# Linear recurrence layer: casts of x and of weights moved from ScalarE to VectorE, and gate weights loaded a step earlier

## The chip, the cores and the metric

One core of one Trainium2 chip runs the whole program. The metric is device microseconds (us) of one execution, as the median of several runs. Five queues work side by side: PE (TensorE, matmuls; PEld its weight loads), DVE (VectorE), ACT (ScalarE), POOL (GpSimd) and SP (SyncE, which here only issues DMAs). Each takes its instructions in a fixed order and stands at the first one that has to wait.

## What is computed

The reference runs four layers over 256 context tokens and 512 latent tokens of width 1024: rwkv7, rglru (a gated linear recurrence), natten, rwkv7. Only the second, rglru, is changed. Cut to its core:

```python
z = h @ w_in                          # 1024 -> 2 * 1408
xr, g = z[..., :1408], z[..., 1408:]
x = depthwise_conv_centred(xr, conv_w, conv_b)     # 4 taps over time
for d in range(2):                    # forward, backward
    r = sigmoid(block_diag(x, gate_w[d, 0]) + gate_b[d, 0])   # 16 blocks of 88
    i = sigmoid(block_diag(x, gate_w[d, 1]) + gate_b[d, 1])
    log_a = -8 * r * softplus(-lam[d])
    a, b = exp(log_a), sqrt(-expm1(2 * log_a)) * (i * x)
    h_d = linear_scan(a, b)           # context first, then latents
y = ((h_0 + h_1) * silu(g)) @ w_out   # 1408 -> 1024
```

## The kernel before

Every large fp32 matmul is made of three. A matrix is split into a high part (a cast to fp32r) and a low part (the source less the high part, cast again), and the sum of high*high, low*high and high*low is taken. So each operand costs a cast (hi) and a subtraction (lo). The helper `split` (L224) does this for activations and gate weights, `load_w` (L208) for projection weights. Before, the cast of both stands on ACT (`nc.scalar.copy`, L227 and L218) and the subtraction on DVE (L230, L221).

The layer has 1408 channels in 11 blocks of 128, all 768 tokens in the free dimension. Names of tiles as the profile shows them: `wr` a raw weight, `wh`, `wl` its parts; `xf` a projection's result, `xc` the convolved x, `xh` its two parts; `ha` the two parts of a halo (rows of the two neighbour blocks that an 88-wide gate block reaches into); `gr` a raw gate weight, `gh`, `glo` its parts; `sg`, `aa` the gates and the recurrence; `gt` the silu gate; `pa`, `pb` PSUM banks (four of each kind).

Two streams of work are written one into the other by `merge` (L130, called at L1536): `projs`, the 22 projection tiles in the order of `LRO` (x0 x1 x2 g0 x3 g1 x4 g2 ... x10 g8 g9 g10), eight k-steps of six matmuls each (L1402), and `units`, six units of two blocks (the last of one). A unit first makes its gates, four steps (block, gate) with two directions each (L1486, then a sigmoid on ACT that empties the banks, L1492), and then its tail: tanh, exp and square root on ACT (L1497, L1502, L1505), then on DVE the products and scans (L1509 to L1516), one addition on POOL (L1518), a product (L1519) and the store of z.

The order on ACT is the order as written (`manual_schedule` of ACT, L1533). The other queues are put in order by a list scheduler, by readiness in its own time model and else as written. `ahead` at the third k-step of a tile (L1398) loads and splits the weight of the next tile. `xtile` (L1405) copies its result out of PSUM on ACT, convolves on DVE (L1416, L1418) and splits x; at every even block it also fetches the halo of the block before by two DMAs and splits it.

`gw_in(i)` (L1456) loads and splits the gate weight of step i; it is called for step i+1 in the middle of step i, between the two directions, two or three DMAs of 128 KB each. Raw gate tiles and raw projection weights share one ring of three buffers (tag `wr`); `gh`, `glo`, `wh` and `wl` have two each. `self.hi_dve = (0, 1)` (L156) and the counter `self.alt` decide in `load_w` where a weight's cast goes: with (0, 1) always to ACT.

After the last unit the output projection (`out_proj`, L373) loads z and its own weights; its first matmul is at L244.

Of the kernel before, what the change touches and what calls it, by code (L numbers as in the profile page):

```python
# [10 lines left out]
F32 = mybir.dt.float32  # L11
# [5 lines left out]
P = 128  # L17
# [107 lines left out]
def run_all(gen):  # L125
    for _ in gen:
        pass
# [22 lines left out]
class Build:  # L150
# [1197 lines left out]
    def rglru(self, li, pv, md, xs, acc, xsp, last):  # L1348

        tc, nc, a = self.tc, self.nc, self.a  # L1350
        NT = 11
        toks = [(0, TC), (TC, TL)]
        HSEG = ((2, TC), (260, TL))
# [32 lines left out]
        self.pq = tc.alloc_tile_pool(name=f"lps{li}", bufs=4, space=bass.MemoryType.PSUM)  # L1386
        order = [(c[0], int(c[1:])) for c in LRO.split()]
        self.plan([(a[f"l{li}_win"][m + NT * (c == "g")], 1024) for c, m in order])
        self.ahead(2)
# [3 lines left out]
        def dense(m):  # L1393
            wh, wl = self.need()
            outs = [self.psa(), self.psa()]
            for kt in range(KT):
                if kt == 2:
                    self.ahead()  # L1398
                ws = slice(kt * 128, kt * 128 + 128)
                for p_i, (wt, xt) in enumerate(((wh, h[kt][0]), (wl, h[kt][0]), (wh, h[kt][1]))):  # L1400
                    for pt, (s0, n) in zip(outs, SEGS):
                        nc.tensor.matmul(pt[:, :n], wt[:, ws], xt[:, s0:s0 + n], start=(kt == 0 and p_i == 0), stop=(kt == KT - 1 and p_i == 2))  # L1402
                yield outs

        def xtile(m):  # L1405

            for outs in dense(m):
                yield 1.0
            xp = self.g("xf")
            for z in (0, 258, 772):  # L1410
                nc.gpsimd.memset(xp[:, z:z + 2], 0.0)
            for pt, o0, n in ((outs[0], 2, TC), (outs[1], 260, TL)):
                nc.scalar.copy(xp[:, o0:o0 + n], pt[:, :n])
            x = xc[m] = self.g("xc")
            cw = lambda j: pv[:, self.LRU_CW + j * NT + m:self.LRU_CW + j * NT + m + 1]
            nc.vector.tensor_scalar(x[:, 2:772], xp[:, 0:770], cw(0), pv[:, self.LRU_CB + m:self.LRU_CB + m + 1], op0=ALU.mult, op1=ALU.add)  # L1416
            for j in range(1, 4):
                nc.vector.scalar_tensor_tensor(out=x[:, 2:772], in0=xp[:, j:j + 770], scalar=cw(j), in1=x[:, 2:772], op0=ALU.mult, op1=ALU.add)  # L1418
            hi, lo = X[m] = self.g("xh", F32R), self.g("xh", F32R)
            self.split(x[:, 2:772], hi[:, 2:772], lo[:, 2:772])  # L1420
            if m and m % 2 == 0:

                r1, r2 = halo(m - 1)
                n, xf = r1 + r2, self.g("xf")
                nc.sync.dma_start(xf[0:r1, 2:772], xc[m - 2][P - r1:P, 2:772])
                nc.sync.dma_start(xf[r1:n, 2:772], x[0:r2, 2:772])
                hi, lo = X["n", m - 1] = self.g("ha", F32R), self.g("ha", F32R)
                self.split(xf[:n, 2:772], hi[:n, 2:772], lo[:n, 2:772])

        first = [xtile(0), xtile(1)]  # L1430

# [10 lines left out]
        def gtile(m):  # L1442

            for outs in dense(NT + m):
                yield 1.0
# [5 lines left out]
        base = [0]  # L1451
        for m in range(NT):
            base.append(base[-1] + len(gate_src(m)))
        GW = {}

        def gw_in(i):  # L1456

            if i < 2 * NT:
                m, gi = divmod(i, 2)
                n = (base[m + 1] - base[m]) * 256  # L1460
                gr = self.wp.tile([P, 768], F32, tag="wr", name=self.nm("gr"), bufs=self.wb[0])
                gh = self.gp.tile([P, 768], F32R, tag="gh", name=self.nm("gh"), bufs=2)
                gl = self.gp.tile([P, 768], F32R, tag="gl", name=self.nm("glo"), bufs=2)
                for s_ in range(base[m + 1] - base[m]):
                    nc.sync.dma_start(gr[:, s_ * 256:s_ * 256 + 256], a[f"l{li}_gw"][base[m] + s_, gi])
                self.split(gr[:, :n], gh[:, :n], gl[:, :n])
                GW[i] = gh, gl

        def unit(ms):

            self.mark(f"unit{ms[0]}")
            keys = [(m, d) for m in ms for d in range(2)]
            R, I, A = {}, {}, {}
            for m in ms:
                srcs = gate_src(m)
                for gi, dstt in ((0, R), (1, I)):
                    if 2 * m + gi == 0:
                        gw_in(0)
                    gh, gl = GW.pop(2 * m + gi)
                    for d in range(2):  # L1480
                        outs = [self.psb(), self.psb()]
                        for si, (key, k) in enumerate(srcs):
                            ws = slice(si * 256 + d * 128, si * 256 + d * 128 + 128)
                            for p_i, (wt, xt) in enumerate(((gh, X[key][0]), (gl, X[key][0]), (gh, X[key][1]))):
                                for pt, (s0, n) in zip(outs, HSEG):
                                    nc.tensor.matmul(pt[:, :n], wt[:k, ws], xt[:k, s0:s0 + n], start=(si == 0 and p_i == 0), stop=(si == len(srcs) - 1 and p_i == 2))  # L1486
                        if d == 0:
                            gw_in(2 * m + gi + 1)
                        o = dstt[m, d] = self.g("sg")
                        cb = self.LRU_GB + (d * 2 + gi) * NT + m  # L1490
                        for pt, (s0, n) in zip(outs, toks):
                            nc.scalar.activation(o[:, s0:s0 + n], pt[:, :n], AF.Sigmoid, bias=pv[:, cb:cb + 1])  # L1492
                        yield float(len(srcs))

            for m, d in keys:
                A[m, d] = self.g("aa")
                nc.scalar.activation(A[m, d][:, :T], R[m, d][:, :T], AF.Tanh, scale=spl[:, d * NT + m:d * NT + m + 1])  # L1497
                for (s0, n), (x0, _) in zip(toks, HSEG):
                    (nc.gpsimd if d else nc.vector).tensor_tensor(out=I[m, d][:, s0:s0 + n], in0=I[m, d][:, s0:s0 + n], in1=xc[m][:, x0:x0 + n], op=ALU.mult)
                yield 0.3  # L1500
            for m, d in keys:
                nc.scalar.activation(R[m, d][:, :T], R[m, d][:, :T], AF.Exp, scale=spn[:, d * NT + m:d * NT + m + 1])  # L1502
                yield 0.3
            for m, d in keys:
                nc.scalar.activation(A[m, d][:, :T], A[m, d][:, :T], AF.Sqrt)  # L1505
            yield 1.0
            for m, d in keys:
                aa, bb, hs = R[m, d], A[m, d], I[m, d]
                nc.vector.scalar_tensor_tensor(out=bb[:, :T], in0=aa[:, :T], scalar=1.0, in1=bb[:, :T], op0=ALU.add, op1=ALU.mult)  # L1509
                nc.vector.tensor_tensor(out=bb[:, :T], in0=bb[:, :T], in1=hs[:, :T], op=ALU.mult)  # L1510
                if d == 0:
                    nc.vector.tensor_tensor_scan(out=hs[:, :T], data0=aa[:, :T], data1=bb[:, :T], initial=0.0, op0=ALU.mult, op1=ALU.add)
                else:
                    rv = lambda ap, s0, n: ap[:, s0:s0 + n][:, ::-1]
                    nc.vector.tensor_tensor_scan(out=rv(hs, 0, TC), data0=rv(aa, 0, TC), data1=rv(bb, 0, TC), initial=0.0, op0=ALU.mult, op1=ALU.add)
                    nc.vector.tensor_tensor_scan(out=rv(hs, TC, TL), data0=rv(aa, TC, TL), data1=rv(bb, TC, TL), initial=hs[:, 0:1], op0=ALU.mult, op1=ALU.add)  # L1516
                    z = I[m, 0]
                    nc.gpsimd.tensor_tensor(out=z[:, :T], in0=z[:, :T], in1=hs[:, :T], op=ALU.add)  # L1518
                    nc.vector.tensor_tensor(out=z[:, :T], in0=z[:, :T], in1=gt[m][:, :T], op=ALU.mult)  # L1519
                    dd = self.dp.tile([P, T], F32, tag=f"z{m}", name=self.nm("zd"))  # L1520
                    nc.sync.dma_start(dd, z[:, :T])
                    zs.append(dd)
                yield 0.3
# [9 lines left out]
        with tc.manual_schedule(engines={mybir.EngineType.Activation}):  # L1533
            for g in first:
                run_all(g)
            merge(projs(), 160.0, [(units(), 104.0 + 25.8) + LRF])  # L1536
        assert len(zs) == NT
        self.close()
        self.pq.release()
        return self.out_proj(li, a[f"l{li}_wout"], zs, NT, md, xsp, last)  # L1540
# [236 lines left out]
def halo(m):  # L1777

    lo, hi = m * P, m * P + P
    return lo % 88 if m else 0, -hi % 88 if m < 10 else 0  # L1780
# [149 lines left out]
AP = 8  # L1930
AB = 4
LRO = "x0 x1 x2 g0 x3 g1 x4 g2 x5 g3 x6 g4 x7 g5 x8 g6 x9 g7 x10 g8 g9 g10"
LRF = (0.10, 1.10)
MH = 7
KB = 2
# [22 lines left out]
```

## Time and profile before

| | |
|---|---|
| median of 3 runs | 3114.08 us (3109.95 to 3116.65) |
| the profiled execution | 3118.23 us, of which its span (first to last instruction) 3116.4 us |
| mean granted TensorE clock over the span | 0.906 of full speed |
| busy over the span | PE 2692.4 us (86%), DVE 1925.0 (62%), ACT 1443.0 (46%), POOL 650.1 (21%) |
| the layer's projections and gates, 1073.46 to 1465.28 us | PE 331.43 us busy, DVE 213.32, ACT 190.67, POOL 51.98; granted clock 0.90 |
| from there to the output projection's first matmuls, 1465.28 to 1493.00 us | PE 0.17 us busy, DVE 11.23, ACT 12.09 |

Times in the profile are microseconds from the span's start. A wait is an engine's idle time just ahead of an instruction, put down to the instruction whose result came last. Two levels of TensorE's clock occur: 1.00 is 2.4 GHz, 0.50 is 1.2 GHz.

### The profile page before, as it was taken

What the parts mean: (1) busy time and instruction counts of PE and PEld (TensorE: products, weight loads), DVE (VectorE), ACT (ScalarE), POOL (GpSimd) and SP (SyncE); (2) the same over time, 40 slices, a digit from 0 to 9 for tenths busy, and PEclk for the clock granted to TensorE, in tenths of its full rate; (3) what the DMA queues carried; (4) which work ended last, traced back from release to release, by engine and by line L of the source; (5) the groups of instructions that cost most, each with busy time, mean ns of one, the idle gap of its engine ahead of it and who ended that gap; (6) DMA issues with size and microseconds to landing.
All of it is one profiled execution on the core that took longest, in us unless ns stands there. A gap on an engine that the chain in (4) does not pass through costs nothing. (4 is left out here: it accounts for less than half of the span.)

```text
span 3116.4 us, 66606 instructions
## 1 busy us (share of the span) xinstructions
PE 2692.4 (86%) x28000; PEld 2195.3 (70%) x28000; DVE 1925.0 (62%) x3291; ACT 1443.0 (46%) x2638; POOL 650.1 (21%) x609
## 2 busy tenths in 40 slices
PE   5999979888887998785889999999798787888886
PEld 3877767777675777674678888877585665777775
DVE  4768797688863445554333434443777877888853
ACT  3444544656562344445234344342454454656561
POOL 1013441121211001111103223220104433121211
PEclk9999889899898999987889999999798888889988
DMA  6235554543427411120741111127224545443423
GB/s 219 92 128 183 184 186 132 153 140 112 130 64 248 145 58 56 61 65 25 275 152 50 47 51 47 46 83 261 77 93 179 194 157 185 143 128 119 135 72 115
DMA packets 170584, 388.78 MB, mean 125 GB/s; under 512 B 20412, under 2 KB 55868, under 8 KB 170284
## 3 DMA queue, kind: packets, MB, share of 16 engines
q1 hardware_dynamic: 170284, 384.52, 37.1%
q8 instruction: 220, 3.60, 0.5%
q14 instruction: 80, 0.66, 0.1%
HBM read 286.06 MB, written 97.65 MB: 123 GB/s over the span
## 5 line engine op out<-in xcount | busy, mean ns | idle before, releaser
L634 PE MATMUL pa<-x,wh 128*128 128x512 f32 (+1 forms) x1552 | 407.1, 370 | 44.0 <-ACT x L227 27.7
L634 PEld LDWEIGHTS pa<-x,wh 128*128 128x128 f32 x1552 | 287.8, 202 | 98.3 <-ACT x L227 32.1
L244 PE MATMUL pa<-z,wh 128*128 128x256 f32 (+1 forms) x992 | 244.4, 358 | 43.1 <-ACT z L227 38.1
L1576 PE MATMUL pa<-h,wh 128*128 128x256 f32 (+1 forms) x1024 | 255.1, 354 | 9.3 <-ACT wh L218 7.2
L221 DVE TENSOR_TENSOR wl<-wr,wh 128x1024 fp32r<-128x1024 f32 (+1 forms) x148 | 186.5, 1262 | 111.0 <-ACT wh L218 110.5
L218 ACT CAST wh<-wr 128x1024 fp32r<-128x1024 f32 (+1 forms) x148 | 158.1, 1068 | 179.9 <-PE pa L244 126.3
L634 PE MATMUL pa<-x,wl 128*128 128x512 f32 (+1 forms) x776 | 231.9, 369 | 5.9 <-DVE wl L221 5.9
L244 PEld LDWEIGHTS pa<-z,wh 128*128 128x128 f32 x992 | 173.8, 193 | 86.4 <-ACT z L227 39.4
L912 DVE TENSOR_TENSOR tmpN<-al,N 128x31 f32<-128x31 f32 (+15 forms) x496 | 213.4, 430 | 14.0
L914 DVE TENSOR_TENSOR N<-N,tmpN 128x31 f32<-128x31 f32 (+15 forms) x496 | 209.7, 423 | 12.8
L1576 PEld LDWEIGHTS pa<-h,wh 128*128 128x128 f32 x1024 | 178.6, 194 | 46.7 <-issue 17.9
L1402 PE MATMUL pa<-h,wh 128*128 128x256 f32 x704 | 168.6, 352 | 15.1 <-ACT wh L218 11.2
L634 PEld LDWEIGHTS pa<-x,wl 128*128 128x128 f32 x776 | 156.2, 204 | 31.3 <-DVE wl L221 7.8
L1402 PEld LDWEIGHTS pa<-h,wh 128*128 128x128 f32 x704 | 126.3, 197 | 38.5 <-ACT wh L218 12.3
L244 PE MATMUL pa<-z,wl 128*128 128x256 f32 (+1 forms) x496 | 139.4, 353 | 0.5 <-DVE wl L221 0.5
L407 DVE SCALAR_TENSOR_TENSOR x<-pa,md,x 128x512 f32<-128x512 f32 (+1 forms) x56 | 33.4, 633 | 167.5 <-PE pa L244 167.5
L227 ACT CAST x<-xf 128x770 fp32r<-128x770 f32 x96 | 80.1, 834 | 122.5 <-DVE xf L528 73.3
L854 PE MATMUL A<-krs,be 64*128 64x128 f32 x1536 | 121.0, 297 | 18.1 <-ACT sc L865 8.1
L1576 PE MATMUL pa<-h,wl 128*128 128x256 f32 (+1 forms) x512 | 135.6, 344 | 0.6 <-DVE wl L221 0.6
L868 DVE TENSOR_TENSOR sc<-A,msk 128x512 f32<-128x512 f32 x128 | 82.7, 686 | 76.1 <-PE A L854 76.0
L854 PEld LDWEIGHTS A<-krs,be 64*128 64x128 f32 x1536 | 102.2, 198 | 33.7 <-ACT sc L865 8.9
L733 POOL TENSOR_SCALAR pcs<-pm 128x12 f32<-128x12 f32 (+2 forms) x48 | 38.5, 813 | 384.5 <-ACT pm L730 372.0
(342 smaller groups left out, 6497.1 us busy)
## 6 DMA issues: line engine op xcount, KB each, us to landing
wr<-in_l_win_dram SPq DMA_DIRECT2D x118, 512.0 KB, 3.8
ar<-in_l_ada_dram SPq DMA_DIRECT2D x88, 512.0 KB, 5.4
krd<-kr SPq DMA_DIRECT2D x32, 768.0 KB, 3.3
bed<-be SPq DMA_DIRECT2D x32, 768.0 KB, 3.6
krs<-krd SPq DMA_DIRECT2D x96, 256.0 KB, 3.2
be<-bed SPq DMA_DIRECT2D x96, 256.0 KB, 3.1
kr<-krd SPq DMA_DIRECT2D x96, 256.0 KB, 3.0
uv<-vn SPq DMA_DIRECT2D x192, 64.0 KB, 2.4
```

The costliest lines, as they stand in the source:

```text
L218: nc.scalar.copy(hi, raw)
L221: lo_eng.tensor_tensor(out=lo, in0=raw, in1=hi.bitcast(F32), op=ALU.subtract)
L227: nc.scalar.copy(hi, src)
L244: nc.tensor.matmul(outs[si][:mw, :n], wt[:kp, ws], xt[:kp, s0:s0 + n], start=(kt == 0 and p_i == 0), stop=(kt == nk - 1 and p_i == 2),)
L634: nc.tensor.matmul(outs[si][:, :n], wt[:, ws], xt[:, s0:s0 + n], start=(first and p_i == 0), stop=(final and p_i == 2))
L733: nc.gpsimd.tensor_scalar(pcs[:, m, o0:o0 + iv.shape[1], d], iv, 1.0, None, op0=ALU.mult)
L854: nc.tensor.matmul(T_["s"][hh][:, c * 128:c * 128 + 128].rearrange("p (s x) -> p s x", s=2), T_["be"][hs, c, :], kv, start=True, stop=True)
L868: y = op("V", 602, pr, [x], lambda h, ov2=ov2, mv=mv, iv=iv: nc.vector.tensor_tensor(out=ov2, in0=iv().rearrange("p (j q x) -> p j q x", j ...
L912: nc.vector.tensor_tensor(out=tv, in0=al[:, i + 1:32, i:i + 1].broadcast_to([P, n, w]), in1=N[:, i:i + 1, 0:w].broadcast_to([P, n, w]), op ...
L914: nc.vector.tensor_tensor(out=N[:, i + 1:32, 0:w], in0=N[:, i + 1:32, 0:w], in1=tv, op=ALU.subtract))
L1402: nc.tensor.matmul(pt[:, :n], wt[:, ws], xt[:, s0:s0 + n], start=(kt == 0 and p_i == 0), stop=(kt == KT - 1 and p_i == 2))
L1576: nc.tensor.matmul(pt[:, :n], wt[:, ws], xt[:, s0:s0 + n], start=(kt == 0 and p_i == 0), stop=(kt == KT - 1 and p_i == 2))
```

## The change

The cast of x, of the halo and of the gate weights is issued on DVE. Within this layer `hi_dve` is (1, 2), so `load_w` puts the cast of every weight with an even count on DVE and leaves the others on ACT; at the layer's end it is set back. `gw_in` is cut in two: `gw_load(i)` issues the DMAs, `gw_in(i)` splits. In step i, between the directions, step i+1's weight is split and step i+2's is loaded. The subtractions, the matmuls and the buffers' numbers stay as they are.

```diff
--- before.py
+++ after.py
@@ -1348,6 +1348,7 @@
     def rglru(self, li, pv, md, xs, acc, xsp, last):
 
         tc, nc, a = self.tc, self.nc, self.a
+        self.hi_dve = HL
         NT = 11
         toks = [(0, TC), (TC, TL)]
         HSEG = ((2, TC), (260, TL))
@@ -1417,7 +1418,7 @@
             for j in range(1, 4):
                 nc.vector.scalar_tensor_tensor(out=x[:, 2:772], in0=xp[:, j:j + 770], scalar=cw(j), in1=x[:, 2:772], op0=ALU.mult, op1=ALU.add)
             hi, lo = X[m] = self.g("xh", F32R), self.g("xh", F32R)
-            self.split(x[:, 2:772], hi[:, 2:772], lo[:, 2:772])
+            self.split(x[:, 2:772], hi[:, 2:772], lo[:, 2:772], hi_eng=nc.vector)
             if m and m % 2 == 0:
 
                 r1, r2 = halo(m - 1)
@@ -1425,7 +1426,7 @@
                 nc.sync.dma_start(xf[0:r1, 2:772], xc[m - 2][P - r1:P, 2:772])
                 nc.sync.dma_start(xf[r1:n, 2:772], x[0:r2, 2:772])
                 hi, lo = X["n", m - 1] = self.g("ha", F32R), self.g("ha", F32R)
-                self.split(xf[:n, 2:772], hi[:n, 2:772], lo[:n, 2:772])
+                self.split(xf[:n, 2:772], hi[:n, 2:772], lo[:n, 2:772], hi_eng=nc.vector)
 
         first = [xtile(0), xtile(1)]
 
@@ -1451,19 +1452,24 @@
         base = [0]
         for m in range(NT):
             base.append(base[-1] + len(gate_src(m)))
-        GW = {}
+        GW, GR = {}, {}
+
+        def gw_load(i):
+
+            if i < 2 * NT:
+                m, gi = divmod(i, 2)
+                gr = GR[i] = self.wp.tile([P, 768], F32, tag="wr", name=self.nm("gr"), bufs=self.wb[0])
+                for s_ in range(base[m + 1] - base[m]):
+                    nc.sync.dma_start(gr[:, s_ * 256:s_ * 256 + 256], a[f"l{li}_gw"][base[m] + s_, gi])
 
         def gw_in(i):
-
             if i < 2 * NT:
                 m, gi = divmod(i, 2)
                 n = (base[m + 1] - base[m]) * 256
-                gr = self.wp.tile([P, 768], F32, tag="wr", name=self.nm("gr"), bufs=self.wb[0])
+                gr = GR.pop(i)
                 gh = self.gp.tile([P, 768], F32R, tag="gh", name=self.nm("gh"), bufs=2)
                 gl = self.gp.tile([P, 768], F32R, tag="gl", name=self.nm("glo"), bufs=2)
-                for s_ in range(base[m + 1] - base[m]):
-                    nc.sync.dma_start(gr[:, s_ * 256:s_ * 256 + 256], a[f"l{li}_gw"][base[m] + s_, gi])
-                self.split(gr[:, :n], gh[:, :n], gl[:, :n])
+                self.split(gr[:, :n], gh[:, :n], gl[:, :n], hi_eng=nc.vector)
                 GW[i] = gh, gl
 
         def unit(ms):
@@ -1475,7 +1481,9 @@
                 srcs = gate_src(m)
                 for gi, dstt in ((0, R), (1, I)):
                     if 2 * m + gi == 0:
+                        gw_load(0)
                         gw_in(0)
+                        gw_load(1)
                     gh, gl = GW.pop(2 * m + gi)
                     for d in range(2):
                         outs = [self.psb(), self.psb()]
@@ -1486,6 +1494,7 @@
                                     nc.tensor.matmul(pt[:, :n], wt[:k, ws], xt[:k, s0:s0 + n], start=(si == 0 and p_i == 0), stop=(si == len(srcs) - 1 and p_i == 2))
                         if d == 0:
                             gw_in(2 * m + gi + 1)
+                            gw_load(2 * m + gi + 2)
                         o = dstt[m, d] = self.g("sg")
                         cb = self.LRU_GB + (d * 2 + gi) * NT + m
                         for pt, (s0, n) in zip(outs, toks):
@@ -1535,6 +1544,7 @@
                 run_all(g)
             merge(projs(), 160.0, [(units(), 104.0 + 25.8) + LRF])
         assert len(zs) == NT
+        self.hi_dve = (0, 1)
         self.close()
         self.pq.release()
         return self.out_proj(li, a[f"l{li}_wout"], zs, NT, md, xsp, last)
@@ -1930,6 +1940,7 @@
 AP = 8
 AB = 4
 LRO = "x0 x1 x2 g0 x3 g1 x4 g2 x5 g3 x6 g4 x7 g5 x8 g6 x9 g7 x10 g8 g9 g10"
+HL = (1, 2)
 LRF = (0.10, 1.10)
 MH = 7
 KB = 2
```

## Rows read from the trace of the kernel before

**Rows 1.** Groups of PE; columns: line, operation, count | busy, mean ns | idle before, releasers.
```profile
L1402 PE MATMUL pa<-h,wh 128*128 128x256 f32 x704 | 168.6, 352 | 15.1 <-ACT wh L218 11.2 <-ACT h L227 3.3 <-POOL h L230 0.2
...
L1486 PE MATMUL pb<-xh,gh 128*128 128x256 f32 x336 | 91.5, 374 | 27.5 <-ACT sg L1492 27.5
L1486 PE MATMUL pb<-xh,glo 128*128 128x256 f32 (+1 forms) x168 | 49.0, 373 | 20.6 <-DVE glo L230 20.6
```

**Rows 2.** Timeline of PE: start, us, instruction, [idle before, releaser].
```profile
1186.70 1.37 PE L1486 MATMUL pb<-xh,gh 128*128 128x256 f32 x2 [9.74 <-ACT sg L1492]
...
1252.38 0.72 PE L1486 MATMUL pb<-xh,glo 128*128 128x256 f32 x2 [3.93 <-DVE glo L230]
...
1265.21 1.01 PE L1402 MATMUL pa<-h,wh 128*128 128x256 f32 x2 [8.21 <-ACT wh L218]
...
1277.95 0.52 PE L1486 MATMUL pb<-xh,gh 128*128 128x256 f32 x2
...
1448.97 2.31 PE L1486 MATMUL pb<-xh,gh 128*128 128x256 f32 x4 [6.68 <-ACT sg L1492]
...
1459.15 1.01 PE L1486 MATMUL pb<-xh,glo 128*128 128x256 f32 x2 [7.86 <-DVE glo L230]
...
1492.83 1.01 PE L244 MATMUL pa<-z,wh 128*128 128x256 f32 x2 [27.56 <-ACT z L227]
```

**Rows 3.** Timeline of ACT at the second border.
```profile
1261.02 0.83 ACT L227 CAST xh<-xc 128x770 fp32r<-128x770 f32 x1 [17.48 <-DVE xc L1418]
...
1264.12 1.04 ACT L218 CAST wh<-wr 128x1024 fp32r<-128x1024 f32 x1
```

**Rows 4.** Waits in the stretch: who for whom, us in total, times, longest.
```profile
ACT xh L227 <- DVE xc L1418: 92.3, 11, 17.7
...
ACT ha L227 <- DMA xf<-xc: 7.9, 5, 2.0
```

**Rows 5.** Timeline of DVE at the second border.
```profile
1237.52 1.83 DVE L1509 SCALAR_TENSOR_TENSOR aa<-sg,aa 128x768 f32<-128x768 f32 x2 [8.96 <-ACT aa L1505]
...
1251.37 0.95 DVE L230 TENSOR_TENSOR glo<-gr,gh 128x768 fp32r<-128x768 f32 x1
...
1259.97 1.02 DVE L1418 SCALAR_TENSOR_TENSOR xc<-xf,pv,xc 128x770 f32<-128x770 f32 x1
```

**Rows 6.** Windows: sum over the eight stretches between 1105.97 and 1409.76 at clock 0.50.
```profile
sum 54.62, PE 38.50 PEld 31.32 DVE 45.21 ACT 24.51 POOL 5.28; mean PE 4.81 PEld 3.92 DVE 5.65 ACT 3.06 POOL 0.66
```

**Rows 7.** Groups of ACT from 1060 to 1480: the casts.
```profile
L218 ACT CAST wh<-wr 128x1024 fp32r<-128x1024 f32 x22 | 23.0, 1044 | 0.0
...
L227 ACT CAST gh<-gr 128x512 fp32r<-128x512 f32 (+1 forms) x22 | 15.3, 699 | 0.0
...
L227 ACT CAST xh<-xc 128x770 fp32r<-128x770 f32 x11 | 9.2, 834 | 92.3 <-DVE xc L1418 92.3
...
L227 ACT CAST ha<-xf 48x770 fp32r<-48x770 f32 x5 | 4.2, 833 | 7.9 <-DMA xf<-xc 7.9
```

**Rows 8.** Line L218 before 1063 us: min/median/max ns.
```profile
L218 ACT CAST wh<-wr x39: 1034/1051/1083, 67.4 to 1039.8; 128x1024 fp32r<-128x1024 f32 x39
```

**Rows 9.** Groups of DVE by form, whole span.
```profile
L693 DVE COPY kk<-rn 128x768 f32<-128x768 f32 x14 | 7.7, 550 | 0.1
...
L230 DVE TENSOR_TENSOR glo<-gr,gh 128x768 fp32r<-128x768 f32 x8 | 7.6, 950 | 1.7 <-ACT gh L227 1.7
```

**Rows 10.** The raw gate tile: its DMA issues on SP.
```profile
L1465 SPq DMA_DIRECT2D gr<-in_l_gw_dram x52: 322/423/573, 1095.7 to 1415.5; - x52
```

**Rows 11.** Timeline, all engines, under a POOL addition.
```profile
1085.85 1.88 POOL L230 TENSOR_TENSOR h<-xf,h 128x768 fp32r<-128x768 f32 x1 [3.02 <-ACT h L227]
1085.86 0.17 DVE L1369 TENSOR_TENSOR st<-st,s 128x22 f32<-128x22 f32 x1
...
1086.06 1.71 DVE L1370 TENSOR_SCALAR st<-st 128x22 f32<-128x22 f32 x1
```

**Rows 12.** DMA issues: KB each, median us to landing.
```profile
wr<-in_l_win_dram SPq DMA_DIRECT2D x118, 512.0 KB, 3.8
```

## The prediction

> **What bounds the kernel now.** Only one of four layers is touched, the linear recurrence, so I looked at its stretch alone, 1073 to 1493 us of the span. First view: TensorE's groups there [rows 1]. The reader is to see the right-hand column: where TensorE waits and on whom. It waits 11.2 us for weight casts on ACT (wh), 27.5 us for gate sigmoids on ACT (sg, which empty the PSUM banks), 20.6 us for the low part of the gate weights on DVE (glo): 59.3 us. Between these waits TensorE is never idle for long, so TensorE sets the end of this stretch, and a wait that goes from this list comes off the time.
>
> Second view: the same waits in order of time [rows 2]. They sit at the borders between two units (a unit is two channel blocks): 9.74 us at 1186.70, 3.93 and 8.21 at 1252.38 and 1265.21, two more borders like these, and at the end 6.68 and 7.86, when no projection is left to cover. Then 27.56 us until the output projection has its first z. By subtraction the end holds 14.5 us, and the four borders with one early wait hold 59.3 - 14.5 = 44.8 us: 3.0 early (wh, 11.2 less 8.21) and 41.8 at the borders, 10.4 each.
>
> Third: why ACT is late. ACT runs in written order. At the second border it finished its work and then stood 17.48 us before the cast of x's high part at 1261.02, because that cast waits for the convolution on DVE; the wh that TensorE wanted follows at 1264.12 [rows 3]. Over the stretch ACT stands 92.3 us before 11 such casts, up to 17.7 at once [rows 4]. Nothing behind the cast needs x; it is only queued behind it.
>
> Fourth: what DVE does then [rows 5]. From 1237.52, when ACT's square roots arrive (DVE stood idle 8.96 us for them), DVE runs its whole unit's tail and the convolution, in one burst until 1260.99. The low part of the gate weights, whose high part comes from ACT only after the square roots, falls into that burst (1251.37), and TensorE waits for it at 1252.38.
>
> Fifth: TensorE's clock. Eight stretches in the waits' wake, 54.62 us, have a granted clock of 0.50, the 1.2 GHz level; TensorE is busy 38.50 us of them [rows 6]. At full clock that work takes half, so 19.2 us are lost here besides the waits.
>
> **The change, part by part.** ACT loses 11 xh casts (9.2 us), 5 ha casts (4.2), 22 gh casts (15.3) and half of 22 wh casts (23.0/2 = 11.5): 40.2 us [rows 7]. Which half matters. 39 weights were cast before [rows 8], so the layer's first is the 40th, even, and goes to DVE; every other one follows: all x tiles but x1, and g9. The tile after each border (x5, x7, x9, g9) is among them; g0, for which TensorE waited early, stays on ACT.
>
> DVE gains the same casts. No cast to fp32r on DVE is in the trace. The nearest row is a DVE copy of one SBUF tile, 550 ns for 128x768; the other bound is the two-input subtraction of the same size, 950 ns [rows 9]. I take the copy (one input, same sizes), scaled by elements over a fixed 0.17 us (a 128x22 DVE instruction [rows 11]): 0.55 us for 770 or 768 columns, 0.42 for 512, 0.68 for 1024. Sum (8 of the 22 gh have three parts, 768 columns): 11 x 0.55 + 5 x 0.55 + 8 x 0.55 + 14 x 0.42 + 11 x 0.68 = 26.6 us; by the other bound 26.6 x 950/550 = 46. DVE is busy 213 of the stretch's first 392 us (table above), so room there is; only what falls into the four bursts counts.
>
> What that buys, border by border. (a) ACT no longer waits for the convolution, so sigmoids and remaining wh casts follow the square roots directly. (b) The gate weights' two parts need only their raw tile, and can be made in DVE's 8.96 us of idle time before the burst: 0.55 + 0.95 us. (c) wh of the tile after the border needs only its raw tile and the buffer of the x tile before it, and can stand there too, or between the burst's dependent instructions. What is late next: the halo part of x (ha). The convolution ends at 1260.99, less 0.95 for the glo that is gone; then cast 0.55, halo copy 2.0 (the longest that ACT waited for it [rows 4]), cast 0.55, subtraction 0.95: about 1264. Its first user's block begins at 1277.95 [rows 2]; 12.1 us of waits and some 3 us of half clock earlier that is about 1263. A low wait of 1 to 3 us stays; I take 2.5 of 10.4 us at each of four borders (bounds: 0, if all hides; 10.4, if DVE is as late as ACT was). Early: wl of g0 stands behind a convolution on DVE; I leave 2.3 of 3.0.
>
> (d) End: the sigmoid wait (6.68) is behind ACT's own tail, no cast, and stays. The glo wait (7.86) goes by (b); I take 7. The 27.56 us after it stay: same chain.
>
> (e) Loading two steps ahead: 52 DMAs of 0.42 us issue on SP [rows 10] move ahead by one step, past a weight load, a halo copy or a z store, all on SP. ACT waited 0.0 us for a raw gate tile in all 22 casts [rows 7], so by itself this is worth nothing before; it serves (b). Each such tile holds one of three raw buffers for a step; a weight load behind it may start later, lands 3.8 us after issue [rows 12], and is issued while at least five of the eight k-steps of the tile before it are still to do: hidden, unless DVE splits the gate tile late (rival three).
>
> (f) Against it stands DVE's sharing with POOL. A 128x22 instruction, 0.17 us, took 1.71 us when it started under a POOL addition, and ended with it (1087.77 against 1087.73) [rows 11]. The Trainium skill, GPSIMD Engine Reference, Key points, says that GpSimd shares its SBUF interfaces with VectorE and contends with DVE instructions in a 2-port mode or with two SBUF inputs. The row agrees; by that rule the new copies are exposed and the same casts on ACT were not. My sum goes without it, since POOL works at the borders mostly where DVE waits for it anyway; with it, rival two.
>
> **Sum.** Borders 41.8 - 10 = 31.8; early 0.7; end 7; clock: waits shrink but some stay, so I let half of 19.2 come back, 9.6. Together 49 us. The profiled execution took 3118.23 us (span 3116.4 and 1.8 around it), so it would be 3069; it is 4.15 above the median 3114.08, so the median becomes **3065 us**. If nothing but the end's 6.68 stayed: 59.3 - 6.7 + 19.2 = 72, so 3042. If each border kept 5 us and the clock nothing: 21.8 + 7 = 29, 3085. Its own range is 3042 to 3085.
>
> **Rivals.**
> One, DVE becomes the bound at the borders: all moved work lands behind the convolution. At the second border wl would be ready at 1260.99 + 0.68 + 1.22 = 1262.9 against the 1265.2 at which TensorE went on: 2.3 us saved per border, 9 in all, and the end's 7: 16 us, 3098 (range 3086 to 3107). For it: the burst, 23.5 us long and taken in order. Against: DVE's idle time before each burst.
> Two, the POOL rule of (f) holds the casts: two additions per burst, up to 1.7 us each, four borders, 13.7 us off the gain: 3079. For it: the held row. Against: most casts may be made when POOL is idle.
> Three, slower: the raw buffers. If the gate tile is split only after the burst (1262.9), the weight load behind it lands 3.8 us later and needs 0.68 + 1.22 more: 1268.6, 3.4 us after the old 1265.2, at four borders 14 us, and no gain at the end: 3128. It decides once a load is issued less than 5.7 us before its tile's first matmul. For it: three buffers, two kinds of loads. Against: the split needs nothing but its tile and can come before the burst.
> Four, no change: the waits go over from ACT to DVE one for one, at the border and at the end, and the added 27 us of DVE eat the rest: 3114.
>
> **Chances.** Forecast 0.50; one 0.24; two 0.08; three 0.10; four 0.08. A measurement tells about 0.2% (6 us) from no change. Faster: 0.50 + 0.24 + 0.08 = 0.82; same 0.08; slower 0.10. The range 3042 to 3105 leaves out three, four and a little of one.
>
> **What would show it.** Right: the xh, ha and gh casts under DVE at 0.4 to 0.6 us; ACT's 92.3 us before xh gone; glo before DVE's burst; waits for sg at borders gone but 6 to 7 us at the end; fewer stretches at 0.50; the first z matmul about 49 us earlier than 1492.83. Wrong: TensorE's idle time named DVE wl, glo or ha at 8 us or more per border (one), DVE casts of 1.5 us and more (two), weight casts waiting for their DMA (three).

## The result and the profile after

The changed kernel takes 3082.81 us (median of 4 runs, 3078.18 to 3087.58); the kernel before, beside it on the same chip, 3115.36 (3109.95 to 3120.54). The ratio is 0.9896, 95% interval 0.9873 to 0.9919: 32.5 us faster. The forecast was 3065, its own range 3042 to 3085: the time lies inside, near the slow end.

The layer's stretch, from its first projection matmul to the output projection's first, went from 419.4 us (1073.46 to 1492.83) to 378.55 (1080.33 to 1458.88): 40.8 less. The first window below is its part up to the last gate matmul; the others are four in it with the clock at the 1.2 GHz level (its first 5.65 us are at that level too). Columns: from:to, length, then the busy us (and instructions) of PE, PEld, DVE, ACT and POOL, the granted clock, the DMA engines' share and GB/s.

```profile
1080.33:1428.61 348.28, 318.89 (x1680) 266.45 (x1680) 236.86 (x305) 156.94 (x238) 61.40 (x66) 0.94 0.19 60
...
1198.62:1208.86 10.24, 7.61 (x22) 5.96 (x23) 10.17 (x13) 1.11 (x2) 2.03 (x2) 0.50 0.44 141
1311.26:1321.49 10.23, 4.26 (x14) 3.68 (x15) 8.54 (x12) 0.00 (x0) 5.00 (x9) 0.50 0.32 104
1379.52:1386.35 6.83, 4.72 (x14) 3.73 (x15) 6.83 (x12) 0.25 (x1) 0.05 (x1) 0.50 0.43 133
1420.48:1427.31 6.83, 5.93 (x18) 5.08 (x19) 5.77 (x7) 3.42 (x7) 1.76 (x1) 0.50 0.00 1
```

TensorE is busy 318.89 us there (331.43 before) with the same 1680 matmuls. The 12.5 us came back from the clock: TensorE was busy 51.2 us at the lower level before and 27.5 after, and half of the difference is 11.9. Its idle time fell from 60.4 (391.82 - 331.43) to 29.4. Behind the last gate matmul there are 30.3 us instead of 27.6. So 31.0 + 12.5 - 2.7 = 40.8.

TensorE's groups after, beside [rows 1]:

```profile
L1403 PE MATMUL pa<-h,wh 128*128 128x256 f32 x704 | 166.8, 350 | 9.4 <-DVE wh L216 5.5 <-ACT h L227 2.7 <-POOL h L230 1.3
L1403 PE MATMUL pa<-h,wl 128*128 128x256 f32 x352 | 93.7, 348 | 12.1 <-DVE wl L221 12.1
L1494 PE MATMUL pb<-xh,gh 128*128 128x256 f32 x336 | 82.1, 346 | 6.2 <-ACT sg L1501 6.2
L1494 PE MATMUL pb<-xh,glo 128*128 128x256 f32 (+1 forms) x168 | 45.1, 348 | 4.2 <-DVE glo L230 4.2
```

The waits for sg went from 27.5 to 6.2 and for glo from 20.6 to 4.2. New is wl, 12.1, and what was ACT's wh is now DVE's, 5.5. In order of time, beside [rows 2]:

```profile
1196.46 0.62 PE L1403 MATMUL pa<-h,wl 128*128 128x256 f32 x2 [0.84 <-DVE wl L221]
...
1201.25 1.01 PE L1494 MATMUL pb<-xh,glo 128*128 128x256 f32 x2 [3.47 <-DVE glo L230]
...
1259.90 0.62 PE L1494 MATMUL pb<-xh,glo 128*128 128x256 f32 x2 [0.78 <-DVE glo L230]
...
1317.23 1.01 PE L1403 MATMUL pa<-h,wl 128*128 128x256 f32 x2 [8.22 <-DVE wl L221]
...
1380.64 1.01 PE L1403 MATMUL pa<-h,wh 128*128 128x256 f32 x2 [5.46 <-DVE wh L216]
1382.64 1.01 PE L1403 MATMUL pa<-h,wl 128*128 128x256 f32 x2 [0.99 <-DVE wl L221]
...
1421.38 0.58 PE L1494 MATMUL pb<-xh,gh 128*128 128x256 f32 x1 [6.17 <-ACT sg L1501]
...
1458.88 1.01 PE L244 MATMUL pa<-z,wh 128*128 128x256 f32 x2 [30.26 <-ACT z L227]
```

The four borders hold 19.8 us (41.8 before), unevenly: 4.3, 0.8, 8.2, 6.5. The reader should ask why the second is nearly free and the third is not. DVE's timeline at the four borders and at the end answers it ([rows 5] before):

```profile
1199.44 1.75 DVE L230 TENSOR_TENSOR glo<-gr,gh 128x512 fp32r<-128x512 f32 x1
...
1221.74 0.56 DVE L229 CAST gh<-gr 128x768 fp32r<-128x768 f32 x1 [3.00 <-PE pb L1494]
...
1230.33 0.69 DVE L216 CAST wh<-wr 128x1024 fp32r<-128x1024 f32 x1 [4.47 <-PE pa L1403]
1231.06 1.23 DVE L221 TENSOR_TENSOR wl<-wr,wh 128x1024 fp32r<-128x1024 f32 x1
1234.49 1.83 DVE L1518 SCALAR_TENSOR_TENSOR aa<-sg,aa 128x768 f32<-128x768 f32 x2 [2.20 <-ACT aa L1514]
...
1257.95 0.41 DVE L229 CAST gh<-gr 128x512 fp32r<-128x512 f32 x1
...
1290.88 0.69 DVE L216 CAST wh<-wr 128x1024 fp32r<-128x1024 f32 x1 [3.15 <-PE pa L1403]
1291.48 1.82 DVE L1518 SCALAR_TENSOR_TENSOR aa<-sg,aa 128x768 f32<-128x768 f32 x2
...
1313.98 1.00 DVE L229 CAST xh<-xc 128x770 fp32r<-128x770 f32 x1
1314.90 2.28 DVE L221 TENSOR_TENSOR wl<-wr,wh 128x1024 fp32r<-128x1024 f32 x1
...
1378.37 1.62 DVE L229 CAST xh<-xc 128x770 fp32r<-128x770 f32 x1
1379.91 0.68 DVE L216 CAST wh<-wr 128x1024 fp32r<-128x1024 f32 x1
...
1438.63 0.96 DVE L1528 TENSOR_TENSOR sg<-sg,gt 128x768 f32<-128x768 f32 x1 [1.98 <-POOL sg L1527]
1439.50 1.82 DVE L1518 SCALAR_TENSOR_TENSOR aa<-sg,aa 128x768 f32<-128x768 f32 x2
```

At the first border glo stands behind the burst and takes 1.75 us where 0.68 is usual. At the second wh and wl both stand before the burst (1234.49). At the third only wh does, released just ahead of it (its buffer came free from the x tile before, 3.15 us of waiting); wl is made 24 us later, and takes 2.28 us instead of 1.23. At the fourth neither got ahead: the buffer of wh came free at 1357.35, 3 us into the burst that began at 1354.30. Each is one DVE instruction of about 1 us, and whether it falls ahead of 22 us of burst or behind it decides a wait of 5 to 8 us. It need not be the whole burst: the third border's wl had its source from 1291.57 and its buffer from 1290.49 on, just as the burst began (1291.48), and inside the fourth burst the wl of another tile does stand (1357.78). That this one stands behind all of it is the list scheduler's order; no run tries another.

What POOL does under the slow instructions, and at the end. L1508 (L1499 before) is the product of a gate and x; for the backward direction it stands on POOL, in two halves:

```profile
1198.07 2.58 POOL L1508 TENSOR_TENSOR sg<-sg,xc 128x256 f32<-128x256 f32 x2
...
1313.14 2.96 POOL L1508 TENSOR_TENSOR sg<-sg,xc 128x256 f32<-128x256 f32 x2
...
1377.00 2.57 POOL L1508 TENSOR_TENSOR sg<-sg,xc 128x256 f32<-128x256 f32 x2
...
1428.96 4.01 POOL L1508 TENSOR_TENSOR sg<-sg,xc 128x256 f32<-128x256 f32 x2 [1.02 <-ACT sg L1501]
```

DVE's moved casts, by form (the prices were taken from [rows 9]):

```profile
L229 DVE CAST xh<-xc 128x770 fp32r<-128x770 f32 x11 | 8.1, 733 | 0.1
L216 DVE CAST wh<-wr 128x1024 fp32r<-128x1024 f32 x11 | 7.6, 691 | 22.2 <-PE pa L1403 18.8 <-DMA wr<-in_l_win_dram 3.3
...
L229 DVE CAST gh<-gr 128x512 fp32r<-128x512 f32 x14 | 5.8, 415 | 10.7 <-PE pb L1494 10.7
...
L229 DVE CAST gh<-gr 128x768 fp32r<-128x768 f32 x8 | 4.9, 615 | 12.5 <-PE pb L1494 10.9 <-DMA wr<-in_l_win_dram 1.6
...
L229 DVE CAST ha<-xf 48x770 fp32r<-48x770 f32 x5 | 2.7, 541 | 0.0
```

ACT after ([rows 4, 7] before): no xh, ha or gh is left on it, and its 92.3 us before xh are gone. Its remaining 11 weight casts now wait for data:

```profile
L218 ACT CAST wh<-wr 128x1024 fp32r<-128x1024 f32 x11 | 11.5, 1049 | 21.5 <-DMA wr<-in_l_win_dram 21.5
```

### The profile page after: what moved, and what is told of

Its sections match the earlier page's. It is cut to its first block, busy times and chain, and to the rows that moved or that the text cites. A ratio compares the mean times of both kernels' runs of the same rounds, so it can differ in the third digit from the quotient of the medians.

```text
span 3085.8 us, 66603 instructions
## 1 busy us (share of the span) xinstructions
PE 2687.9 (87%) x28000; PEld 2192.8 (71%) x28000; DVE 1958.7 (63%) x3340; ACT 1408.5 (46%) x2589; POOL 662.0 (21%) x609
## 5 line engine op out<-in xcount | busy, mean ns | idle before, releaser
L218 ACT CAST wh<-wr 128x1024 fp32r<-128x1024 f32 (+1 forms) x137 | 146.6, 1070 | 204.3 <-PE pa L244 118.7
L1403 PEld LDWEIGHTS pa<-h,wh 128*128 128x128 f32 x704 | 125.2, 195 | 32.5 <-DVE wh L216 5.8
```

Source lines behind the costliest of these rows:

```text
L218: nc.scalar.copy(hi, raw)
```

## The experiments

Each edit is made to the changed kernel. Times are medians, ratios are to the kernel before, timed beside it on the same chip. "Stretch" is as above (before 419.4, changed 378.55). No kernel leaves out work. How finely the stretch can be read: the first and the fifth below, whose waits are those of their partners, differ from them by 0.4 and 2.2 us.

**The load.** First with only the two-ahead load undone:

```diff
+                gw_load(i)
                 gr = GR.pop(i)
...
-                            gw_load(2 * m + gi + 2)
```

> The changed kernel, but with each gate weight loaded where it is split, one step ahead as before; all casts stay on DVE. Theory A, the earlier load is what lets the gate weights of a border's second step be split before DVE's burst: without it TensorE waits 3 to 8 us for the low gate parts at some borders, stretch 383 to 395. Theory B, the load was never late and the split is placed by its buffers: stretch within 3 us of 378.6.

3079.79 us, ratio 0.9871 [0.985, 0.9892]; stretch 378.9, the same waits at the same places (theory B). The earlier load does nothing.

**One kind of cast back on ACT at a time.** x and the halo:

```diff
-            self.split(x[:, 2:772], hi[:, 2:772], lo[:, 2:772], hi_eng=nc.vector)
+            self.split(x[:, 2:772], hi[:, 2:772], lo[:, 2:772])
```

(the halo's the same)

> The changed kernel, but with the casts of x and of its halo back on ACT; gate and half of the projection weights stay on DVE. The stretch meant is from the layer's first projection matmul to the first matmul of the output projection: 419.4 us before, 378.6 us after the change. Theory A, ACT's in-order wait for the convolution (92.3 us before) is what made TensorE wait at the borders: the stretch goes back to 400 to 412 us, the time to 3103 to 3113, and ACT's waits of up to 17 us ahead of the x cast are there again. Theory B, what counts is ACT's load, the number of casts: x and halo are 13.4 of 40.2 us, so a third of the gain goes, stretch about 392.

3077.8 us, 0.9868 [0.985, 0.9887]; stretch 381.8. Both expected stretches missed. ACT stands 91.5 us before xh again, as it did before the change, and TensorE's four borders read 3.23 (sg), 3.70 (sg), 9.40 (wl), 6.75 (wh). ACT's long stand, which the prediction made the cause, costs about 3 us once the other casts are off ACT.

The gate weights:

```diff
-                self.split(gr[:, :n], gh[:, :n], gl[:, :n], hi_eng=nc.vector)
+                self.split(gr[:, :n], gh[:, :n], gl[:, :n])
```

> The changed kernel, but with the casts of the gate weights back on ACT; x, halo and half of the projection weights stay on DVE. Theory A, the gate weights' high parts must be made on DVE to get their low parts ahead of DVE's burst: the waits for the low gate parts come back, 3 to 4 us at three or four borders and 8 us at the end, stretch 393 to 400. Theory B, with ACT no longer standing before the x cast its gate casts come early enough anyway: stretch within 3 us of 378.6.

3082.8 us, 0.988 [0.9856, 0.9904]; stretch 381.4. TensorE's group in that run:

```profile
L1494 PE MATMUL pb<-xh,glo 128*128 128x256 f32 (+1 forms) x168 | 47.6, 366 | 22.9 <-DVE glo L230 22.9
```

The glo waits are back (20.6 before, 4.2 in the changed kernel), 3.5 to 4.1 at each border and 7.85 at the end, and yet the stretch grew by only 3, as theory B had it: the waits for wh and wl went.

The weights:

```diff
-HL = (1, 2)
+HL = (0, 1)
```

> The changed kernel, but with all projection weight casts on ACT. Theory A, the weight of the tile after a border is made ahead of DVE's burst only if its cast is on DVE; on ACT it follows the square roots, and its low part then stands behind the burst: 6 to 8 us of wait for wl at each of four borders instead of 19.8 us in all, stretch 385 to 395. Theory B, ACT is free now, so it does not matter where this half is cast: stretch within 3 us of 378.6.

3084.22 us, 0.9885 [0.9864, 0.9907]; stretch 382.1, between the two that were expected.

```profile
L1403 PE MATMUL pa<-h,wl 128*128 128x256 f32 x352 | 94.6, 351 | 27.0 <-DVE wl L221 27.0
```

Now it is wl at every border (6.21, 6.96, 7.87, 5.62).

So three different things end last in three kernels, at nearly one time. By the time of the whole program none of the three can be told from the change: all four intervals overlap. The 3 us are a reading of the stretch alone.

**One kind of cast alone.** The load alone, all casts on ACT (the three edits above together):

> The earlier load of the gate weights alone; every cast on ACT as before. Both theories: the load was never late, so the stretch stays within 3 us of the 419.4 us of before. It is also the base of the three runs beside it. Theory C (borders have several chains that end within a few us of each other: taking out any one of the three cast groups from the change costs only 3 us) and theory D (each group is worth the 3 us that it costs to take it out) differ in those.

3120.84 us, 1.0008 [0.9993, 1.0023]; stretch 417.2, the waits of the kernel before, as both theories had it.

With it, x and halo alone on DVE (the second and third edit):

> The earlier load, and of the casts those of x and its halo alone on DVE; gate and projection weights cast on ACT. Theory C: ACT no longer stands before the convolution, which was the longest chain at three borders; the low gate parts (3 to 4 us a border, 8 at the end) and wl are left: stretch 388 to 398. Theory D: 3 us less than the load alone, about 416.

3087.83 us, 0.9908 [0.9882, 0.9935]; stretch 386.9, just under theory C's 388 to 398. The waits are nearly all glo's: 11.53, 3.58, 3.97, 3.76 at the borders, 7.85 at the end.

The gate weights alone (the first and third):

> The earlier load, and of the casts those of the gate weights alone on DVE; x, halo and projection weights cast on ACT. Theory C: the 8 us at the end go and the low gate parts at the borders, but the sigmoids still stand behind ACT's wait for the convolution: stretch 393 to 405. Theory D: 3 us less than the load alone, about 416.

3099.62 us, 0.9944 [0.9925, 0.9963]; stretch 398.5, inside theory C's 393 to 405. The glo waits are gone, at the end too; the borders read 8.92 (sg), 10.33 (wh on ACT), 9.0 and 7.42 (sg).

Every other wh alone (the first two):

> The earlier load, and of the casts half of the projection weights' alone on DVE; x, halo and gate weights cast on ACT. Theory C: of the three chains only the weight's is gone, and it was the last one at one border alone: stretch 405 to 414. Theory D: 3 us less than the load alone, about 416.

3093.58 us, 0.9924 [0.9899, 0.9948]; stretch 391.9, far under the 405 to 414 expected. ACT still stands 98.1 us before xh, but at the first border TensorE's wait for sg is 3.13 instead of 9.74. ACT in the kernel before, and then DVE, ACT and TensorE in this run, show why:

```profile
1180.83 0.83 ACT L227 CAST xh<-xc 128x770 fp32r<-128x770 f32 x1 [10.13 <-DVE xc L1418]
```

```profile
1169.37 0.69 DVE L216 CAST wh<-wr 128x1024 fp32r<-128x1024 f32 x1 [5.33 <-DMA wr<-in_l_win_dram]
1170.10 1.23 DVE L221 TENSOR_TENSOR wl<-wr,wh 128x1024 fp32r<-128x1024 f32 x1
1172.73 1.83 DVE L1518 SCALAR_TENSOR_TENSOR aa<-sg,aa 128x768 f32<-128x768 f32 x2 [1.41 <-ACT aa L1514]
...
1185.81 0.84 ACT L227 CAST xh<-xc 128x770 fp32r<-128x770 f32 x1 [10.16 <-DVE xc L1419]
...
1192.72 0.54 PE L1494 MATMUL pb<-xh,gh 128*128 128x256 f32 x1 [3.13 <-ACT sg L1501]
```

ACT stands as long as before, and TensorE's gates go on 20.0 us after the start of DVE's burst (18.9 before). But the weight of the next projection tile (x5) is split ahead of the burst, so TensorE works on that tile until 1189.59. Before, it ran out of work at 1176.96 (1186.70 less 9.74), since that weight, too, stood behind ACT's wait.

Against 417.2 the three alone gain 30.3, 18.7 and 25.3 us: 74.3 in sum, where all together gain 38.6; taken out one by one they cost 3.3, 2.9 and 3.6. So theory D is out: the gains do not add. Theory C came near for x and gates and missed for wh, and its picture of several chains that TensorE must all wait for does not fit either: then one alone would gain little, and one put back would cost nearly everything. TensorE's waits (of 0.3 us and more, in us) in the eight kernels, all with the earlier load, show what happens:

| casts on DVE | the four borders | the end |
|---|---|---|
| none | 41.8 | 14.5 |
| x and halo | 25.3 | 14.5 |
| gate weights | 38.0 | 6.2 |
| every other wh | 20.0 | 14.5 |
| gate weights and wh | 24.0 | 6.2 |
| x, halo and wh | 15.5 | 14.5 |
| x, halo and gate weights | 26.7 | 6.2 |
| all | 19.8 | 6.2 |

The 8.4 us at the end belong to the gate weights, whatever else is moved. At the borders wh alone takes off 21.8 us, as much as all three, x 16.5, and both together 26.3. TensorE has two streams there, gates and projections, and in the kernel before both stand behind ACT's wait. Moving x takes that wait away; moving wh takes the projections out from behind it, and the trace above shows them covering the gates' wait. So each does much of the other's work. With the gate casts moved beside another kind, the borders are 1 to 4 us longer; so the change without them costs only 2.9 us, 8.4 more at the end and 4.3 less at the borders among it.

One thing is mixed in: the list scheduler orders TensorE's matmuls anew for each edit. The orders of the kernel before and of the load alone are the same, and so are those of the changed kernel, of the load undone and of the addition moved (below); between the changed kernel and the one before some 50 of the stretch's 1680 matmuls stand elsewhere (outside the longest order that both have, by tile names and shapes), in the other kernels 14 to 115 against the changed one. How much of each single share is order was not separated.

**The other half of the weights.**

```diff
-        if self.alt % self.hi_dve[1] < self.hi_dve[0]:
+        if (self.alt + (self.hi_dve == HL)) % self.hi_dve[1] < self.hi_dve[0]:
```

> The changed kernel with the other half of the projection weights cast on DVE (counts that are odd: x1 and the g tiles but g9) and the x tiles and g9 on ACT. Theory A, at the borders only the tile after the border matters (x5, x7, x9, g9): its weight now comes from ACT after the square roots, its low part stands behind DVE's burst, and TensorE waits 5 to 8 us for wl at all four borders, as with every cast on ACT (382.1 us): stretch 380 to 385. Theory B, any half relieves both engines alike: waits for weights at two borders as in the changed kernel, stretch 376 to 380.

3086.75 us, 0.989 [0.9862, 0.9917]; stretch 381.9, in the 380 to 385 expected. wl is late at all four borders (5.28, 7.52, 6.49, 4.46). Which half is worth 3 us, hardly more than the reading's fineness.

**The POOL addition.** Each burst holds two dependent additions on POOL (L1527), for each of which DVE stands. Moved to DVE:

```diff
-                    nc.gpsimd.tensor_tensor(out=z[:, :T], in0=z[:, :T], in1=hs[:, :T], op=ALU.add)
+                    nc.vector.tensor_tensor(out=z[:, :T], in0=z[:, :T], in1=hs[:, :T], op=ALU.add)
```

> The changed kernel with the addition of the two directions' scans (one per block) on DVE and no longer on POOL. Theory P, POOL's additions lengthen DVE's burst, by DVE's wait for each (1.7 us) and by holding DVE instructions beside them: each burst is 1.5 to 4 us shorter, the weight waits behind it shrink by as much, stretch 367 to 375. Theory Q, DVE's own work is what fills the burst: the 0.95 us of each addition take the place of the 1.7 us of waiting, stretch within 3 us of 378.6.

3067.0 us, 0.9822 [0.9798, 0.9845]; stretch 364.1, under the 367 to 375 expected, with TensorE's order unchanged. Its third border on DVE:

```profile
1280.86 1.82 DVE L1518 SCALAR_TENSOR_TENSOR aa<-sg,aa 128x768 f32<-128x768 f32 x2
...
1299.75 0.95 DVE L1527 TENSOR_TENSOR sg<-sg,sg 128x768 f32<-128x768 f32 x1
1300.62 0.56 DVE L229 CAST xh<-xc 128x770 fp32r<-128x770 f32 x1
...
1303.29 1.22 DVE L221 TENSOR_TENSOR wl<-wr,wh 128x1024 fp32r<-128x1024 f32 x1
```

From burst to xh there are 19.8 us (22.5 in the changed kernel), and xh takes 0.56 instead of 1.00, wl 1.22 instead of 2.28. TensorE still waits 6.18 for wl there, and 3.42 and 1.30 at the fourth border. The window up to the last gate matmul:

```profile
1077.34:1413.04 335.70, 313.57 (x1680) 262.74 (x1680) 240.24 (x314) 156.98 (x238) 64.18 (x57) 0.96 0.20 62
```

Of the 14.4 us gained, 7.3 are idle time (29.4 to 22.1), 5.3 the clock (318.89 to 313.57), 1.8 the end.

**Weight parts off DVE.** All wh on ACT (HL as above) and the wl of every other weight on POOL (`lo_pool` is set behind the layer's first two weights and taken back at its end; these lines are left out here):

```diff
         if lo_eng is None:
-            lo_eng = nc.vector
+            lo_eng = nc.gpsimd if self.lo_pool and self.alt % 2 == 0 else nc.vector
```

> The changed kernel with all projection weight casts on ACT, and from the layer's third weight on the low part of every other one (x tiles and g9, the tiles after the borders) made on POOL. x, halo and gates stay on DVE. Theory W, what TensorE now waits for at the borders is the low weight part behind DVE's burst (26.7 us at four borders when all casts are on ACT): those waits go, what comes next is 3 us or less a border, stretch 352 to 366. Theory R, other chains end at the same place (gates, halo), or POOL's subtraction holds DVE's burst up by sharing: stretch 370 to 382.

3080.13 us, 0.9868 [0.9844, 0.9892]; stretch 378.4, as without the edit. At the third and fourth border nothing waits for weight parts any more, and TensorE waits for gh there instead (3.43, 3.30). DVE and POOL in the second burst:

```profile
1234.84 3.42 DVE L1527 TENSOR_TENSOR_SCAN sg<-sg,sg,aa 128x512 f32<-128x512 f32 x1
...
1239.04 2.59 DVE L1520 SCALAR_TENSOR_TENSOR aa<-sg,aa 128x768 f32<-128x768 f32 x1
```

```profile
1234.57 2.61 POOL L222 TENSOR_TENSOR wl<-wr,wh 128x1024 fp32r<-128x1024 f32 x1 [16.02 <-ACT wh L219]
1238.34 2.47 POOL L1529 TENSOR_TENSOR sg<-sg,sg 128x768 f32<-128x768 f32 x1 [1.16 <-DVE sg L1527]
```

The scan takes 1.28 us where POOL is idle, 3.42 here under POOL's subtraction; the aa product, 0.93 otherwise, takes 2.59 under POOL's addition. Theory R holds.

**Both together.** The last two edits:

> The change with both of the last two edits: the addition of the two scans on DVE, all casts of projection weights on ACT, and every other weight's subtraction on POOL. With the addition alone on DVE the stretch was 364.1 us and TensorE still waited 11 us at two borders for weight parts from DVE; with the weight parts off DVE alone it was 378.4 us, and the waits went to gate parts, while POOL's subtraction of 1024 columns stretched a DVE instruction from 1.28 to 3.42 us. Theory W (what is left after the addition is moved is the weight parts queued on DVE): these waits go, no other chain stands close behind, stretch 350 to 358 us, time 3052 to 3061 us. Theory R (the other chains end close behind, and POOL's subtraction gives back part of what the addition gave): the waits turn to DVE gh and glo, stretch 360 to 370 us, time 3063 to 3073 us, no better than the addition alone. I hold R the likelier, 60 to 40.

3068.7 us, 0.9841 [0.982, 0.9863]; stretch 368.3, R again: no better than the addition alone.

```profile
1080.43:1421.65 341.22, 321.94 (x1680) 268.72 (x1680) 241.00 (x291) 166.03 (x248) 98.09 (x67) 0.95 0.20 61
```

TensorE is idle 19.3 us here against 22.1, but busy 321.94 against 313.57: up to the last gate matmul its clock is at the lower level for 35.7 us against 25.8. At the borders it has seven waits of 10.0 us in sum, where the addition alone has four of 12.3: more and shorter waits, and more time at the lower clock. That their number makes the difference was not tried.

## Why the prediction came out as it did

The direction held, and the mechanism in the main: waits at the borders went, the clock gave part of its loss back. The terms, as the prediction put them, in the profiled pair:

| term | predicted | measured |
|---|---|---|
| borders, 41.8 us less what stays | 31.8 (10 stay) | 22.0 (19.8 stay) |
| early | 0.7 | 1.3 (1.18 and 0.47 stay of 3.0) |
| end, sg and glo | 7 | 8.4 (6.17 stays of 14.5) |
| clock | 9.6 | 12.5 |
| the tail behind the last gate matmul | 0 | -2.7 |

These sum to 41.5, beside 40.8 measured in the stretch (some short waits are left out). The clock's 9.6 was half of what the windows at the borders lost; the same windows gave back 11.0 (TensorE busy 38.50 us in them before, 16.59 after), the rest came at the end and elsewhere. The mis-sized term is what stays at the borders, 19.8 us and not 10.

**(a)** ACT no longer waits for the convolution: seen. That this stand must go for the waits to go fell: with x back on ACT it returned and cost 3 us, and with wh alone on DVE it stayed and the borders still lost 21.8 us. What mattered was what is queued behind it.

**(b)** Held, at every border and at the end. The parts that TensorE had waited for at the second border (glo of 768 columns at 1251.37 [rows 5], inside the burst) are made from 1221.74 on, 13 us ahead of the burst (1234.49); the same parts stand 11 to 14 us ahead of it at the other borders and at the end. But the prediction said that they "need only their raw tile" and forgot the destination: DVE waits for gh buffers that TensorE frees, 3.00 us there, 10.7 + 10.9 over the stretch (groups above). That cost nothing here. It shows in the step after: its gh buffer comes free at 1240.87, inside the burst, its gh stands behind the burst (1257.95), and TensorE waits 3.47 us for such a glo at the first border and 0.78 at the second, where it had other matmuls until 1259.12.

**(c)** Right about the two places, wrong about what is late next. It named the halo (ha) at 2.5 us per border; ha held TensorE nowhere for 0.3 us or more in the changed kernel. Late are projection weights, wh and wl, 15.5 of the 19.8 us, nearly all for the tile after the third and the fourth border: the price taken had wh ahead of the burst or inside it and passed over the subtraction behind it. Rival one had that place for wl, and at the third and fourth border it is what happened; 8.22 us at the third reaches the 8 us that the prediction had named as a sign against itself, at one border of four.

**(d)** The end held for glo (7.86 gone) and sg (6.68 to 6.17). "The same chain" after it did not: with the end 8 us shorter, DVE is still in the unit before (1438.63) when the last square roots end (1437.07), so the last burst begins 10.9 us after the last gate matmul (1439.50 less 1428.61), where it was 7.8 (1473.04 less 1465.28). POOL's product beside it took 4.01 us.

**(e)** Worth nothing by itself: shown, both ways (stretch 378.9 without it, 417.2 with it alone). That it serves (b) fell.

**(f)** Left out of the sum, on the ground that POOL works mostly where DVE waits for it. That looked at POOL's additions and passed over its products (L1508). The xh casts take 0.733 us on average (0.55 priced), 1.00 and 1.62 at the last two borders under a POOL product, 0.589 when the additions are on DVE. The sharing is in the rows; moving the additions gave 14.4 us, but that edit also takes away DVE's stands for them (19.5 us in all ahead of 11 products, 1.7 to 2.0 each), so the share of each is not settled. The prices themselves were near: 29.1 us of casts against 26.6.

**Rival two** named 3079, nearest to the result, but not for its reason. It had POOL's two additions per burst holding the new casts, 13.7 us. The casts together took 2.5 us more than priced, and those held at the last two borders (xh 0.45 and 1.07 us over its 0.55) stood beside POOL's product, not an addition. So did the wl of the third border (1.05 over 1.23), the glo of the first (1.75 where 0.68 is usual) and DVE's L1528 at the first and fourth (1.38 each for 0.96). Together that is some 4.5 of the 9.8 us by which the borders missed; the rest fits wh and wl standing behind the burst.

**Rival three.** Its mechanism came, on ACT: 21.5 us of waiting for raw weights, twice, up to 12.2. The longer follows the late wl of the third border, which frees a raw buffer (the load is issued at 1317.20), and not a late gate tile. No matmul waited behind it. **Rival four** fell with 22 us gone from the borders.

**The rest of the program.** The span lost 30.6 us where the stretch lost 40.8: 6.9 came ahead of the stretch and 3.3 behind it, in layers that the change does not touch. Over the fourteen profiled executions the stretch began between 1071.7 and 1080.4, and 1619 to 1629 us followed it, so one execution can carry that much; why the changed kernel's lay high is open. The kernel with the load undone, the same in its waits, gave 0.9871, and its interval (0.985 to 0.9892) overlaps that of the change.

## What to carry to other kernels

When TensorE has two streams of work and stands at a border, ask for each stream what would have let it go on. Here a ready projection covered the gates' wait, and three moves that gained 19 to 30 us each alone gained 39 together, and each could be put back for 3. Add such shares only after trying each move alone and each put back. In this kernel a 1 us instruction got ahead of a burst only where its source and its destination buffer were both free before it, and what came free a moment after its start often stood behind the whole of it; look up who frees the buffer. And when work is moved to an engine, look first at what that engine stands for inside its burst: moving one addition off POOL was worth more than any of the three casts was at the margin.

## What the hardware showed that was not expected

DVE and POOL slow each other, and which of them loses changes. A DVE scan of 1.28 us took 3.42 under a POOL subtraction. POOL's product (L1508, two halves, some 1.9 us before) took 2.96 at the third border of the changed kernel while DVE's xh and wl beside it took 1.00 and 2.28; with the additions moved, POOL's took 7.76 while DVE ran from 1300.62 on without a gap and its xh and wl took 0.56 and 1.22:

```profile
1300.15 7.76 POOL L1508 TENSOR_TENSOR sg<-sg,xc 128x256 f32<-128x256 f32 x2
```

POOL's spans are rough, but DVE's are not. What decides who waits was not tried.

The Trainium skill, GPSIMD Engine Reference, Key points, says that GpSimd shares its SBUF interfaces with VectorE and names the two kinds of DVE instructions that contend; the rows agree, with the scan's 3.42 us (two inputs) and the xh cast's 1.00 and 1.62. The same section calls DVE about twice as fast for elementwise work; here the addition took 0.95 us on DVE and 1.80 on POOL where nothing ran beside it, 2.4 within a burst, which agrees.
